# A decoder layer on TensorE: the streamed and the stationary matmul operands are given one address modulo 2048 bytes

## The chip, the core and the metric

The kernel runs on one core of a Trainium2 chip. The metric is the device time of one execution in microseconds (us). Every instruction below is named by its engine (PE is TensorE's matmul, PEld its weight load, DVE VectorE, ACT ScalarE, POOL GpSimd, SP SyncE) and its line in the kernel.

## The reference

One layer on 256 tokens with 2048 channels, all float32. The input is normalised and projected to ten parts; two mixers run side by side, 16-head latent attention with a rotary part, and a short causal convolution; each is widened by a SiLU path, projected back to 2048 channels and weighted by a sigmoid gate computed from the input; the sum goes through one more 2048 x 2048 projection, a norm and the residual.

```python
h = _rmsnorm(x, pre_norm_g)
proj = jnp.einsum('bsd,de->bse', h, w_in)
# split: q_a, c_kv, k_rope, z_mla, c_in, b_gate, c_gate, z_conv, g_mla, g_conv
q  = jnp.einsum('bsr,re->bse', _rmsnorm(q_a, q_a_norm_g), w_q_b)
kv = jnp.einsum('bsr,re->bse', _rmsnorm(c_kv, kv_a_norm_g), w_kv_b)
...
attn = _causal_mla_attention(q_nope, q_rope, k_nope, k_rope, v)
y_mla = jnp.einsum('bse,ed->bsd', attn * silu(z_mla), w_o_mla)
u = c_gate * c_in
conv = sum(conv_w[k] * u_pad[:, k:k + s] for k in range(CONV_K))
y_conv = jnp.einsum('bse,ed->bsd', b_gate * conv * jax.nn.silu(z_conv), w_o_conv)
merged = jax.nn.sigmoid(g_mla) * y_mla + jax.nn.sigmoid(g_conv) * y_conv
out = jnp.einsum('bsd,de->bse', merged, w_out)
return x + _rmsnorm(out, post_norm_g)
```

## The kernel before

**Number format.** A float32 factor is kept as two fp32r parts, a high one (`hi`) and the rest (`lo`), so that one exact product is three matmuls: hi x hi, hi x lo, lo x hi. Activations are stored with both parts side by side: `x_both`, `at_both`, `cv_both` and `m_both` have 16 rows of 512 elements per partition, 256 tokens of the high part and 256 of the low. A row is 2048 bytes. Weights arrive by DMA from SP's queue in units of 128 x 2048 elements (`raw`, three buffers) and are split into `whi` and `wlo`, half a unit (1024 elements, 4096 bytes) at a time, by ACT (line 207) and DVE (line 208), five buffers each.

**Order of the work.** First the input is scaled and split into `x_both` and projected to the latents `qa` and `ckv`. Then comes a loop over 16 heads: five projections of `x_both` per head (`z`, `cg`, `ci`, `b`, `c`), with the attention of the head woven in (`qn`, `kn`, `qr`, `vv`, `sc`, `tp`, `o`). Its results lie in `at_f` and `cv_f`, which are then split into `at_both` and `cv_both`. Then four blocks of 512 output columns (`c` from 0 to 3); in each, four products of 256 tokens by 512 columns are made by `tokens`: two gates from `x_both`, then `at_both` with the attention's output weights, then `cv_both` with the convolution's. Each such product takes 16 rows x 2 halves of the tokens x 3 = 96 matmuls of 512 columns. `features` turns the merged block into `m_both`. Last, four more blocks of 96 matmuls (`out`) multiply `m_both` by the output weights, and each is followed by its part of the norm (`out_block`, `row_norm`, `finish`).

**Which operand streams.** A matmul instruction has a stationary operand, which a weight load brings in before, and a moving one, whose 512 (or 256) columns are then streamed. In `halves`, which makes the heads' projections (lines 202 and 204), the weights are stationary and a whole row of `x_both` streams. In `product` (lines 194 to 196), which makes the `sq` and `out` blocks, it is the other way round: 128 tokens of the activation are stationary (512 bytes per partition) and 512 columns of weights stream (2048 bytes).

```python
def product(ps, a, b, first, last):
    (ah, al), (bh, bl) = a, b
    nc.tensor.matmul(ps, ah, bh, start=first, stop=False)
    nc.tensor.matmul(ps, ah, bl, start=False, stop=False)
    nc.tensor.matmul(ps, al, bh, start=False, stop=last)
```

**Where the tiles lie.** Pools are stacks in each partition's memory: `const` and `wpool` grow from the low end, and `hp`, `cp`, `op` follow on them; `top`, `fp`, `bp`, later `merged_pool` and `dp`, come from the high end down. The size of what is put on first therefore sets the address of all that follows. `LINE` is 32 elements, 128 bytes, and the pads `top_pad` and `const_pad` bring the tiles to multiples of that. The scheduler lays out the order of the instructions on each engine; the weights' buffers come free as the matmuls that read them end.

Of the kernel before, what the change touches and what calls it, by code (L numbers as in the profile page):

```python
# [11 lines left out]
F32 = mybir.dt.float32  # L12
# [6 lines left out]
P = 128  # L19
S = 256  # L20
NT = S // P
# [12 lines left out]
MASKED = -3e38  # L34

UNIT = 2048
LINE = 32
# [41 lines left out]
def tile_layer(ctx: ExitStack, tc: tile.TileContext, xt, x, pos, pvec, post_g, wqa, wi, wkr, wqk, wrv, wsq, out):  # L79
    nc = tc.nc  # L80

    const = ctx.enter_context(tc.tile_pool(name="const", bufs=1))
    top = ctx.enter_context(tc.tile_pool(name="top", bufs=1, side="right"))
    top.tile([P, LINE - 8], F32, name="top_pad")
    wpool = ctx.enter_context(tc.tile_pool(name="wpool", bufs=1))
    psum = ctx.enter_context(tc.tile_pool(name="psum", bufs=1, space=PSUM))

# [131 lines left out]
    make_identity(nc, ident[:, :])  # L219
    ones = const.tile([P, P], F32, name="ones")  # L220
    nc.gpsimd.memset(ones[:, :], 1.0)
    mask = const.tile([P, 3 * P], F32, name="mask")
    nc.gpsimd.memset(mask[:, :], 0.0)
    for o in (0, 2 * P):
        make_causal_mask(nc, mask[:, o : o + P], mask_val=MASKED)
    mhalf = const.tile([P, 1], F32, name="mhalf")
    nc.gpsimd.memset(mhalf[:, :], -0.5)
    hpi = const.tile([P, 1], F32, name="hpi")
# [6 lines left out]
    const.tile([P, LINE - 8], F32, name="const_pad")  # L235
    cos_t = const.tile([P, S], F32, name="cos_t")
    sin_t = const.tile([P, S], F32, name="sin_t")


    main = ctx.enter_context(ExitStack())  # L240
    hp = main.enter_context(tc.tile_pool(name="hp", bufs=1))
    x_both = hp.tile([P, KD, 2 * S], F32R, name="x_both")
    r_x = hp.tile([P, S], F32, name="r_x")
    r_col = hp.tile([P, LINE], F32, name="r_col")[:, :NT]
    fstack = main.enter_context(ExitStack())
    fp = fstack.enter_context(tc.tile_pool(name="fp", bufs=1, side="right"))
    at_f = fp.tile([P, H, S], F32, name="at_f")
# [2 lines left out]
    bp = bstack.enter_context(tc.tile_pool(name="bp", bufs=1, side="right"))  # L250
    qa = bp.tile([P, KR, 2 * S], F32R, name="qa")
    ckv = bp.tile([P, KR, 2 * S], F32R, name="ckv")
    kr = bp.tile([P, 2, S], F32R, name="kr")

    xs = at_f
    angles = [at_f[:, H - 1 - i, :] for i in range(5)]
# [339 lines left out]
    bp = cp  # L596
# [65 lines left out]
    op = ctx.enter_context(tc.tile_pool(name="op", bufs=1))  # L662
# [2 lines left out]
    gb = op.tile([P, D], F32, name="gb")  # L665
    nc.scalar.dma_start(out=gb[:, :], in_=post_g.to_broadcast([P, D]))
    nc.scalar.dma_start(out=xr[:, :, :], in_=x)
    ssq = op.tile([P, NT, LINE // 2], F32, name="ssq")

    def out_products(ps, t, w, kk):  # L670
        ts = slice(t * P, (t + 1) * P)
# [4 lines left out]
    def out_block(c, t, ps):  # L676
        cs = slice(512 * c, 512 * c + 512)
        junk = op.tile([P, 512], F32, name=f"junk{c}_{t}", tag="junk", bufs=2)
        nc.scalar.activation(junk[:, :], ps[:, :], AF.Square, accum_out=ssq[:, t, c : c + 1])
        if c == 3:  # L680
            rr = row_norm(t)
        nc.vector.tensor_tensor(og[:, t, cs], ps[:, :], gb[:, cs], op=ALU.mult)
        return rr if c == 3 else None

    last = []
    part = op.tile([P, LINE], F32, name="part")[:, :NT]

    def row_norm(t):

        ss = op.tile([P, LINE], F32, name=f"fss{t}")[:, :1]  # L690
        nc.vector.scalar_tensor_tensor(
            ss[:, :], ssq[:, t, 3:4], 1.0 / D, part[:, t : t + 1], op0=ALU.mult, op1=ALU.add
        )
        rr = op.tile([P, LINE], F32, name=f"frr{t}")[:, :1]
        nc.gpsimd.tensor_tensor(rr[:, :], ss[:, :], mhalf[:, :], op=ALU.pow)
        return rr

# [111 lines left out]
```

## Time and profile before

| | us |
|---|---|
| median of three runs | 1079.74 |
| the three runs | 1077.57, 1079.74, 1079.75 |
| the profiled execution | 1077.44 |
| its span, first to last instruction | 1075.6 |
| granted TensorE clock over the span | 0.997 |

The span is what the trace shows; 1.8 us of the execution's time lie around it. A row of the profile gives a group of instructions with its count, its busy time and what ended the engine's idle time before it. Ends of matmuls are modelled (a 512-column one is always shown as about 0.39 us long and overlaps the next), so the pace of a stream of matmuls is read from start to start, or from a stretch's length divided by the number of matmuls that start in it.

### The profile page before, as it was taken

To read this page: it belongs to the slowest core of one execution; us is meant where nothing else is said; L and a number is where in the kernel's file an instruction comes from. 1 tells how busy PE (TensorE), PEld (TensorE's weight loads), DVE (VectorE), ACT (ScalarE), POOL (GpSimd) and SP (SyncE) were. 2 spreads that over 40 slices of the span, in tenths; PEclk is the share of its full clock that TensorE was granted. 3 is DMA by queue.
4 is the path that set the end of the run, shared out by engine and by line. 5 is a ranking of instruction groups with operands and counts; after the bars stand their busy time and mean duration, and the time that the engine had idled before them with its cause. 6 is when DMAs were issued, how large, how long until landed. Compare 5 with 4: busy or idle time off the path is not lost.

```text
span 1075.6 us, 14368 instructions
## 1 busy us (share of the span) xinstructions
PE 1056.0 (98%) x5576; PEld 907.3 (84%) x5576; DVE 729.6 (68%) x1132; ACT 586.9 (55%) x849; POOL 47.6 (4%) x70
## 2 busy tenths in 40 slices
PE   9988999999999999999999999999999999999997
PEld 7877798888889889888888878888888888888885
DVE  6999897877877778878787774554455445445562
ACT  7656666666666666666566674334434434434450
POOL 0591000000000000000000000000000000000000
PEclk9999999999999999999999999999999999999998
DMA  8644445454545545545455446555555555557552
GB/s 313 222 146 169 173 161 184 161 195 174 192 169 186 183 160 196 191 152 179 166 194 196 161 161 217 178 190 190 196 195 176 188 187 193 196 194 278 199 189 78
DMA packets 31604, 199.80 MB, mean 186 GB/s; under 512 B 3632, under 2 KB 5296, under 8 KB 9264
## 3 DMA queue, kind: packets, MB, share of 16 engines
q1 hardware_dynamic: 30960, 195.57, 51.4%
q10 hardware_dynamic: 576, 3.31, 0.8%
q8 instruction: 43, 0.70, 0.3%
q14 instruction: 25, 0.20, 0.1%
HBM read 196.78 MB, written 2.10 MB: 185 GB/s over the span
## 4 chain that ended last, share of the span: by engine, by line
PE 86%; DVE 5%; POOL 4%; issue 2%; DMA 2%; ACT 0%; SPq 0%; POOLq 0%; DVEq 0%; ACTq 0%
PE sq L195 11%; PE sq L196 11%; PE sq L194 10%; PE b L202 5%; PE z L202 5%; PE cg L202 5%; PE c L202 5%; PE ci L202 5%; PE c L204 3%; PE b L204 3%; PE ci L204 3%; PE z L204 3%; PE cg L204 3%; PE out L196 2%; PE out L194 2%; PE out L195 2%
## 5 line engine op out<-in xcount | busy, mean ns | idle before, releaser
L208 DVE TENSOR_TENSOR wlo<-raw,whi 128x1024 fp32r<-128x1024 f32 (+1 forms) x372 | 443.0, 1207 | 232.4 <-ACT whi L207 199.0
L207 ACT ACTIVATE whi<-raw 128x1024 fp32r<-128x1024 f32 (+1 forms) x374 | 386.8, 1038 | 338.2 <-PE sq L196 185.5
L195 PE MATMUL sq<-wlo,x_both 128*128 128x512 f32 x256 | 99.7, 390 | 1.6 <-DVE wlo L208 1.6
L196 PE MATMUL sq<-whi,x_both 128*128 128x512 f32 x256 | 99.7, 389 | 0.0
L194 PE MATMUL sq<-whi,x_both 128*128 128x512 f32 x256 | 99.2, 390 | 0.0
L202 PE MATMUL z<-x_both,whi 128*128 128x512 f32 x256 | 61.1, 391 | 2.4 <-DVE f L326 2.4
L202 PE MATMUL b<-x_both,whi 128*128 128x512 f32 x256 | 62.5, 396 | 0.0
L202 PE MATMUL ci<-x_both,whi 128*128 128x512 f32 x256 | 61.5, 392 | 0.0
L202 PE MATMUL cg<-x_both,whi 128*128 128x512 f32 x256 | 61.3, 391 | 0.0
L202 PE MATMUL c<-x_both,whi 128*128 128x512 f32 x256 | 61.1, 391 | 0.0
L195 PEld LDWEIGHTS sq<-wlo,x_both 128*128 128x128 f32 x256 | 48.1, 188 | 11.9 <-DVE wlo L208 2.0
L202 PEld LDWEIGHTS z<-x_both,whi 128*128 128x128 f32 x256 | 47.1, 188 | 11.8 <-issue 2.6
L196 PEld LDWEIGHTS sq<-whi,x_both 128*128 128x128 f32 x256 | 48.1, 188 | 10.0
L194 PEld LDWEIGHTS sq<-whi,x_both 128*128 128x128 f32 x256 | 48.1, 188 | 9.8
L202 PEld LDWEIGHTS b<-x_both,whi 128*128 128x128 f32 x256 | 46.9, 188 | 9.5
L202 PEld LDWEIGHTS c<-x_both,whi 128*128 128x128 f32 x256 | 47.0, 188 | 9.1
L202 PEld LDWEIGHTS cg<-x_both,whi 128*128 128x128 f32 x256 | 46.9, 188 | 9.1
L202 PEld LDWEIGHTS ci<-x_both,whi 128*128 128x128 f32 x256 | 47.0, 188 | 9.1
L196 PE MATMUL sq<-whi,cv_both 128*128 128x512 f32 x128 | 50.5, 395 | 0.0
L194 PE MATMUL sq<-whi,at_both 128*128 128x512 f32 x128 | 50.5, 395 | 0.0
L194 PE MATMUL sq<-whi,cv_both 128*128 128x512 f32 x128 | 50.5, 395 | 0.0
L195 PE MATMUL sq<-wlo,at_both 128*128 128x512 f32 x128 | 50.5, 395 | 0.0
(239 smaller groups left out, 1839.5 us busy)
## 6 DMA issues: line engine op xcount, KB each, us to landing
raw<-wi_dram SPq DMA_DIRECT2D x84, 1024.0 KB, 4.8
raw<-wsq_dram SPq DMA_DIRECT2D x80, 1024.0 KB, 4.8
raw<-wqk_dram SPq DMA_DIRECT2D x8, 1024.0 KB, 4.8
raw<-wrv_dram SPq DMA_DIRECT2D x8, 768.0 KB, 4.1
raw<-wqa_dram SPq DMA_DIRECT2D x8, 256.0 KB, 5.0
raw<-wqa_dram SPq DMA_DIRECT2D x4, 512.0 KB, 7.3
xr<-x_dram ACTq DMA_DIRECT2D x1, 2048.0 KB, 13.3
out_dram<-og SPq DMA_DIRECT2D x6, 256.0 KB, 2.3
```

Source lines behind the costliest of these rows:

```text
L194: nc.tensor.matmul(ps, ah, bh, start=first, stop=False)
L195: nc.tensor.matmul(ps, ah, bl, start=False, stop=False)
L196: nc.tensor.matmul(ps, al, bh, start=False, stop=last)
L202: nc.tensor.matmul(ps[:, :], w[0], both, start=first, stop=False)
L204: nc.tensor.matmul(ps[:, :S], w[1], both[:, :S], start=False, stop=last)
L207: nc.scalar.activation(hi, src, AF.Copy)
L208: nc.vector.tensor_tensor(lo, src, hi.bitcast(F32), op=ALU.subtract)
```

## The change

No instruction is added or removed on any engine but one wait of POOL, and the order on PE, ACT, DVE and SP's queue is the same. What differs is the place of tiles. The mask (1536 bytes) leaves `const` for `bp`, and its memory-set and causal fills on POOL now stand behind the small constants. `r_x` and `r_col` go from `hp` to `const`. The last norm's small tiles (`ssq`, `part`, `fss`, `frr`) go from `op` to `top`, and `top_pad` becomes 480 bytes. With that the addresses within a partition, as the built programs have them, are these:

| tile | before | mod 2048 | mod 512 | after | mod 2048 | mod 512 |
|---|---|---|---|---|---|---|
| `raw`, `whi`, `wlo` (ring) | 21632 on | 1152 | 128 | 21248 on | 768 | 256 |
| `x_both` | 87168 | 1152 | 128 | 86784 | 768 | 256 |
| `at_both` | 121088 | 256 | 256 | 119552 | 768 | 256 |
| `cv_both` | 153856 | 256 | 256 | 152320 | 768 | 256 |
| `m_both` | 196480 | 1920 | 384 | 195328 | 768 | 256 |
| weights of the last `out` block | 132480 on | 1408 | 384 | 131840 on | 768 | 256 |
| `qa`, `ckv`, `kr` | 128256 on | 1280 | 256 | 125568 on | 640 | 128 |
| `qn`, `kn`, `qr`, `vv`, `p` | 161664 on | 1920 | 384 | 160512 on | 768 | 256 |
| `pt` | 193408 | 896 | 384 | 192256 | 1792 | 256 |
| `ident` | 16832 | 448 | 448 | 16832 | 448 | 448 |

```diff
     top = ctx.enter_context(tc.tile_pool(name="top", bufs=1, side="right"))
-    top.tile([P, LINE - 8], F32, name="top_pad")
+    ssq = top.tile([P, NT, LINE // 2], F32, name="ssq")
+    part = top.tile([P, LINE], F32, name="part")[:, :NT]
+    row_s = [top.tile([P, LINE], F32, name=f"fss{t}")[:, :1] for t in range(NT)]
+    row_r = [top.tile([P, LINE], F32, name=f"frr{t}")[:, :1] for t in range(NT)]
+    top.tile([P, 120], F32, name="top_pad")
...
-    mask = const.tile([P, 3 * P], F32, name="mask")
-    nc.gpsimd.memset(mask[:, :], 0.0)
-    for o in (0, 2 * P):
-        make_causal_mask(nc, mask[:, o : o + P], mask_val=MASKED)
     mhalf = const.tile([P, 1], F32, name="mhalf")
...
     sin_t = const.tile([P, S], F32, name="sin_t")
+    r_x = const.tile([P, S], F32, name="r_x")
+    r_col = const.tile([P, LINE], F32, name="r_col")[:, :NT]
...
     x_both = hp.tile([P, KD, 2 * S], F32R, name="x_both")
-    r_x = hp.tile([P, S], F32, name="r_x")
-    r_col = hp.tile([P, LINE], F32, name="r_col")[:, :NT]
...
     kr = bp.tile([P, 2, S], F32R, name="kr")
+    mask = bp.tile([P, 3 * P], F32, name="mask")
+    nc.gpsimd.memset(mask[:, :], 0.0)
+    for o in (0, 2 * P):
+        make_causal_mask(nc, mask[:, o : o + P], mask_val=MASKED)
...
-    ssq = op.tile([P, NT, LINE // 2], F32, name="ssq")
-    part = op.tile([P, LINE], F32, name="part")[:, :NT]
     def row_norm(t):
-        ss = op.tile([P, LINE], F32, name=f"fss{t}")[:, :1]
+        ss, rr = row_s[t], row_r[t]
...
-        rr = op.tile([P, LINE], F32, name=f"frr{t}")[:, :1]
```

## The prediction

> **What bounds the kernel now.** I read the page first: how busy each engine is, the clock, and the chain that ended last.
>
> ```profile
> PE 1056.0 (98%) x5576; PEld 907.3 (84%) x5576; DVE 729.6 (68%) x1132; ACT 586.9 (55%) x849; POOL 47.6 (4%) x70
> PEclk9999999999999999999999999999999999999998
> PE 86%; DVE 5%; POOL 4%; issue 2%; DMA 2%; ACT 0%; SPq 0%; POOLq 0%; DVEq 0%; ACTq 0%
> ```
>
> TensorE is never without work for long, its clock is granted nearly in full throughout, and 86% of the chain is matmuls. So the time is the number of matmuls times their pace, and a change that leaves every engine's instructions and order as they are can only act through the pace of single instructions. The change moves addresses; the question is whether the pace knows of addresses.
>
> Next I cut the second half into its blocks of 96 matmuls, from the first start of one to the first start of the next. The columns are the stretch and its length, PE's busy time (with the rows that touch the stretch, so one or two neighbours are counted too), clock, DMA share and GB/s. First the eight blocks whose stationary operand is `at_both` or `cv_both`:
>
> ```profile
> 667.76:690.07 22.31, 22.31 (x97) 1.00 0.52 188
> 690.07:712.39 22.32, 22.32 (x97) 1.00 0.54 189
> 756.82:779.13 22.31, 22.31 (x97) 1.00 0.53 189
> 779.13:801.45 22.32, 22.32 (x97) 1.00 0.53 188
> 845.88:868.19 22.31, 22.31 (x97) 1.00 0.52 189
> 868.19:890.51 22.32, 22.32 (x97) 1.00 0.54 188
> 934.94:957.25 22.31, 22.31 (x97) 1.00 0.53 189
> 957.25:979.57 22.32, 22.32 (x97) 1.00 0.53 188
> sum 178.52, PE 178.52; mean PE 22.32
> ```
>
> Then blocks of the same shape on `x_both` (the first three) and on `m_both`:
>
> ```profile
> 712.39:734.17 21.78, 21.78 (x98) 1.00 0.56 193
> 801.45:823.23 21.78, 21.78 (x98) 1.00 0.56 194
> 890.51:912.29 21.78, 21.78 (x98) 1.00 0.55 193
> 1002.31:1024.07 21.76, 21.76 (x97) 1.00 0.54 194
> 1024.07:1045.83 21.76, 21.76 (x97) 1.00 0.53 194
> ```
>
> A block on `at_both` or `cv_both` takes 22.31 us, that is 22.31/96 = 232.4 ns a matmul; one on `x_both` 21.78 us (226.9 ns), on `m_both` 21.76 us (226.7 ns). PE is busy without a gap in all of them, at the full clock, on the same instructions with the same shape, and the slow and the fast blocks alternate. The rows of starts show that the difference is in every matmul and not in a wait at some place:
>
> ```profile
> 770.31 0.39 PE L195 MATMUL sq<-wlo,at_both 128*128 128x512 f32 x1
> 770.54 0.39 PE L196 MATMUL sq<-whi,at_both 128*128 128x512 f32 x1
> 770.77 0.39 PE L194 MATMUL sq<-whi,at_both 128*128 128x512 f32 x1
> 770.31 0.19 PEld L196 LDWEIGHTS sq<-whi,at_both 128*128 128x128 f32 x1
> ```
>
> The weight load for the next matmul starts together with the present one (both at 770.31). While one address range streams, another is loaded. So what I look at is their distance: the address of the operand being loaded less that of the one streaming, modulo 512 (successive stationary slices lie 512 bytes apart, so only this remainder is the same for a whole block). From the table of addresses: `x_both` blocks 128 - 128 = 0; `m_both` 384 - 128 = 256; `at_both` and `cv_both` 256 - 128 = 128. Distances 0 and 256 go at 226.7 to 226.9 ns, distance 128 at 232.4.
>
> A third sample comes from the heads, where the weights are the stationary operand. `kn` streams `ckv` while loading `whi`: 128 - 256 = 384 modulo 512. The heads' own projections stream `x_both` at distance 0:
>
> ```profile
> 174.07 1.09 PE L202 MATMUL kn<-ckv,whi 128*128 128x512 f32 x4
> 175.00 0.63 PE L204 MATMUL kn<-ckv,wlo 128*128 128x256 f32 x4
> 175.47 0.28 PE L483 MATMUL sc<-kn,qn_hi 128*128 128x256 f32 x1
> 396.83 3.82 PE L202 MATMUL cg<-x_both,whi 128*128 128x512 f32 x16
> 400.49 2.08 PE L204 MATMUL cg<-x_both,wlo 128*128 128x256 f32 x16
> 402.40 0.86 PE L202 MATMUL ci<-x_both,whi 128*128 128x512 f32 x3
> ```
>
> `kn`: (175.00 - 174.07)/4 = 232.5 ns, as slow as `at_both`. `cg`: (400.49 - 396.83)/16 = 228.8 ns, between the two. The narrow ones (256 columns) go at 0.47/4 = 117.5 ns and 1.91/16 = 119.4 ns: there the distance makes no difference of that kind.
>
> **The change, part by part.**
>
> *`at_both` and `cv_both`* come to distance 256 - 256 = 0 from the weights. Eight blocks of 22.31 become blocks of 21.76 to 21.78: 178.52 - 8 x 21.77 = 4.4 us less, or 178.52 - 8 x 21.78 = 4.3 us; I take 4.3, since `x_both` at distance 0 is the nearest case. The upper bound is 4.4. The lower bound is the pace of `cg`, also at distance 0: 768 x (232.4 - 228.8) = 2.8 us. I take the other end, because the `cg` run follows narrow matmuls and these blocks follow wide ones, as the `x_both` blocks do.
>
> Is the gain passed on to the end? The blocks are PE from end to end, so what is late next would be the weights:
>
> ```profile
> SPq L137 <- DVE wlo L208: 247.6, 48, 5.9
> ACT whi L207 <- PE sq L196: 26.7, 15, 3.1
> raw<-wsq_dram SPq DMA_DIRECT2D x80, 1024.0 KB, 4.8
> ```
>
> SP's queue waits for DVE's split to free a buffer (247.6 us between 712 and 979 us), and ACT waits for PE to free `whi` (26.7 us in two slow blocks). Both are held back by PE, not the reverse, and a unit lands 4.8 us after its issue where a block's quarter lasts 5.4 us. The `x_both` blocks already run at the new pace with the same feed. So all of the 4.3 us reaches the end.
>
> *`x_both`, `m_both`, the last `out` weights.* Distances: `x_both` 0 before and after; `m_both` 256, now 0; the last block 384 - 384 = 0, stays. By the rows of 21.76 and 21.78, 0 to 0.1 us. Taken as 0.
>
> *`qa` and `ckv`* keep a distance: with the weights stationary it goes from 384 to 256 - 128 = 128, and where `ckv` is stationary (`vv`) from 128 to 384. By the rows of 232.4 (128) and 232.5 (384) these are one class: 0. The bounds: `qn`, `kn` and `qr` have 160 wide matmuls; at the fast pace they would save 160 x 5.7 = 0.9 us, and I allow as much the other way, since no row shows this pairing at 128.
>
> ```profile
> L202 PE MATMUL kn<-ckv,whi 128*128 128x512 f32 x64 | 18.3, 399 | 0.6 <-DVE ckv L208 0.5
> L202 PE MATMUL qn<-qa,whi 128*128 128x512 f32 x64 | 17.5, 396 | 0.0
> L202 PE MATMUL qr<-qa,whi 128*128 128x512 f32 x32 | 8.8, 395 | 0.0
> L518 PE MATMUL tp<-ident,p 128*128 128x128 f32 x48 | 8.1, 272 | 0.0
> L629 PE MATMUL mt<-ident,sg 128*128 128x128 f32 x32 | 4.3, 272 | 0.0
> ```
>
> *Transposes* (`tp`, `mt`, 80 of them) go from 384 - 448 = 448 to 256 - 448 = 320, in either role an odd distance before and after: 0, with 80 x 5.7 = 0.5 us either way.
>
> *The mask and the small constants.* POOL's memory-set and two fills of the mask now follow the small constants.
>
> ```profile
> 2.11 0.54 POOL masks.py:30 TENSOR_SCALAR_AFFINE_SELECT mask<-mask 128x128 f32<-128x128 f32 x2
> 2.47 0.20 ACT L231 ACTIVATE warm<-mhalf 128x1 f32<-128x1 f32 x1
> 3.19 0.51 ACT L277 ACTIVATE x_both<-at_f,pv 128x256 fp32r<-128x256 f32 x1 [0.52 <-DMA pv<-pvec_dram]
> ```
>
> ACT's first work waits for the constants' DMA until 3.19 us, after `warm`; the mask is ready at 2.65 us here, and is first read in the heads' loop, behind the whole input stage. 0. *The last norm:* its tiles exist from the start instead of on ground that `cv_both` leaves, so POOL loses a wait for PE that was over long before its wait for DVE. 0.
>
> The sum is -4.3 us, with bounds 4.4 + 0.1 + 0.9 + 0.5 = 5.9 us faster and 2.8 - 0.9 - 0.5 = 1.4 us faster. From the profiled execution's own 1077.44 us that gives 1073.1; from the median of the runs, 1079.74, it gives 1075.4. The four executions lie in two pairs 2.2 us apart; I expect the new median between the two values and write 1074.5.
>
> **The rivals.**
>
> *The address plays no part.* Then the time stays between 1077.4 and 1079.7. [...] The trace does not agree: 22.31 against 21.78 us, eight times over, with nothing else different that I can name. Against that stands that correlation in one execution is all I have; the blocks also differ in their data. 9 in 100.
>
> *A multiple of 256 is what is slow, not the distance.* Before, the slow pairs are those with one operand on a multiple of 256 (`at_both`, `cv_both`, `qa`, `ckv`), and all fast ones are 128 off it. The trace cannot separate this from distance, since no block had both operands on such a multiple. After the change all of them have: the activations, the weights, `m_both`. Then nothing is gained, and every fast wide matmul slows to 232.4 ns: 768 in `sq` on `x_both`, 384 in `out`, 1280 in the heads, 144 in the latents and `kr`, together 2576 x 5.6 = 14.4 us, giving 1091.9 to 1094.1. It decides from 2.2/2576 = 0.9 ns a matmul. For it: the same rows. Against it: `qa` is slow as the streaming operand and `at_both` as the stationary one, which a relation of the two explains with one rule, as it does that distance 256 is fast. 6 in 100.
>
> *Something small that I have not seen eats the gain,* a phase of weight loads as in `cg`, or a later start: about 1077.5. 3 in 100.
>
> **How the numbers follow.** The forecast keeps 82 in 100 and gives 1074.5. Its range goes from the greatest gain below the lower pair, 1077.4 - 5.9 = 1071.5, to 1077.5, the lower pair untouched; that takes in a gain of only 2.8 us from the higher pair, 1079.7 - 2.8 = 1076.9. The measurement can tell about 0.2%, 2.2 us, from no change. Faster by more than that: the forecast, 0.82 with a little of the last rival, 0.83. Same: the first rival and the rest, 0.11. Slower: the second, 0.06.
>
> **What would show it.** Right: the eight blocks last 21.76 to 21.78 us, a sum near 174.2 instead of 178.5; the blocks on `x_both` and `m_both` keep theirs; `kn` keeps 232 ns. Wrong: the eight blocks still last 22.3 us (no part in it), or the `x_both` blocks grow to 22.3 as well (multiples of 256), or they shorten and the span does not follow, with new idle time of PE before them.

## The result and the profile after

| | before | after |
|---|---|---|
| median | 1079.63 us (4 runs, 1077.57 to 1079.75) | 1074.46 us (4 runs, 1073.26 to 1074.65) |
| ratio after to before | | 0.9954, 95% interval 0.9937 to 0.9971 |
| the profiled execution, its span | 1077.44, 1075.6 | 1074.65, 1072.9 |

The kernel became faster by about 0.5%. A later set of five runs of the kernel after, beside nine of before, gave 0.9961 (0.9948 to 0.9975).

The page of after, the same lines as for before (busy time, clock, chain by engine):

```profile
PE 1054.6 (98%) x5576; PEld 909.6 (85%) x5576; DVE 728.8 (68%) x1132; ACT 587.2 (55%) x849; POOL 48.0 (4%) x70
PEclk9999999999999999999999999999999999999999
PE 86%; DVE 5%; POOL 4%; issue 2%; DMA 2%; ACT 0%; SPq 0%; POOLq 0%; DVEq 0%; ACTq 0%
```

Counts and shares are as they were; the bound is the same. The stretches of the eight blocks on `at_both` and `cv_both` in the kernel after (length, PE busy, clock, DMA share, GB/s):

```profile
669.56:691.32 21.76, 21.76 (x97) 1.00 0.55 193
691.32:713.08 21.76, 21.76 (x97) 1.00 0.57 194
757.49:779.25 21.76, 21.76 (x97) 1.00 0.55 194
779.25:801.01 21.76, 21.76 (x97) 1.00 0.56 193
845.43:867.19 21.76, 21.76 (x98) 1.00 0.55 194
867.19:888.95 21.76, 21.76 (x98) 1.00 0.56 193
933.36:955.12 21.76, 21.76 (x98) 1.00 0.54 194
955.12:976.88 21.76, 21.76 (x98) 1.00 0.55 192
sum 174.08, PE 174.08; mean PE 21.76
```

The sum was 178.52 before: 4.44 us less. Blocks on `x_both` (first) and `m_both` (second) of after, and the starts inside a block on `at_both`:

```profile
713.08:734.85 21.77, 21.77 (x98) 1.00 0.55 193
999.59:1021.35 21.76, 21.76 (x97) 1.00 0.56 196
```

```profile
770.64 0.39 PE L199 MATMUL sq<-wlo,at_both 128*128 128x512 f32 x1
770.87 0.39 PE L200 MATMUL sq<-whi,at_both 128*128 128x512 f32 x1
771.09 0.39 PE L198 MATMUL sq<-whi,at_both 128*128 128x512 f32 x1
```

The blocks that hold nothing but their 96 matmuls are now alike, 226.7 ns a matmul, with PE busy from end to end. The gain lies where the prediction put it.

The two profiled spans differ by only 2.8 us although the blocks lost 4.4. The rest lies ahead of them: the execution of after is 1.80 us late at the start of the first of the eight blocks (669.56 us against 667.76). Some 0.5 us of that is lost before `rb_qa` starts (71.61 us against 71.06), and the greater part after it, in the first head, where the clock dips in the execution of after and not in that of before. First before, then after, the same two stretches:

```profile
69.00:92.00 23.00, 18.98 (x111) 1.00 0.37 129
92.00:124.00 32.00, 28.71 (x173) 1.00 0.51 182
```

```profile
69.00:92.00 23.00, 20.01 (x109) 0.93 0.36 126
92.00:124.00 32.00, 28.75 (x157) 0.95 0.52 187
```

A mean clock of 0.93 and 0.95 is two stretches of 3.4 us at half clock, near 72 and 113 us: the granted clock is 0.50 from 71.8 to 75.2 us and from 112.7 to 116.1 us. The first falls on `ci` and is mostly hidden, since `rb_ckv` then waits 0.4 us for DVE instead of 2.0. The second falls on the second head's `z` and costs 1.6 us: its 16 wide matmuls take 117.31 - 111.99 = 5.32 us, in before 115.22 - 111.47 = 3.75. The waits of PE ahead of the two dips are as long as before, to 0.1 us, and the kernel before with a single pad, the first experiment, shows dips in the same two stretches of its profile (mean clock 0.85 and 0.95, over the span 0.993); so I do not put them down to the change. The run named "kept awake" below takes this up.

### The profile page after: what moved, and what is told of

It reads as the page before. It is cut to its first block, busy times and chain, and to the rows that moved or that the text cites. A ratio compares the mean times of both kernels' runs of the same rounds, so it can differ in the third digit from the quotient of the medians.

```text
span 1072.9 us, 14367 instructions
## 1 busy us (share of the span) xinstructions
PE 1054.6 (98%) x5576; PEld 909.6 (85%) x5576; DVE 728.8 (68%) x1132; ACT 587.2 (55%) x849; POOL 48.0 (4%) x70
## 4 chain that ended last, share of the span: by engine, by line
PE 86%; DVE 5%; POOL 4%; issue 2%; DMA 2%; ACT 0%; SPq 0%; POOLq 0%; DVEq 0%; ACTq 0%
PE sq L199 10%; PE sq L200 10%; PE sq L198 10%; PE z L206 5%; PE cg L206 5%; PE ci L206 5%; PE c L206 5%; PE b L206 5%; PE c L208 3%; PE b L208 3%; PE z L208 3%; PE ci L208 3%; PE cg L208 3%; PE out L200 2%; PE out L198 2%
## 5 line engine op out<-in xcount | busy, mean ns | idle before, releaser
L200 PE MATMUL out<-whi,m_both 128*128 128x512 f32 x128 | 49.9, 390 | 0.0
L198 PE MATMUL out<-whi,m_both 128*128 128x512 f32 x128 | 49.9, 390 | 0.0
L199 PE MATMUL out<-wlo,m_both 128*128 128x512 f32 x128 | 49.8, 389 | 0.0
```

## The experiments

**The kernel before, with `at_both` and `cv_both` at distance 256.** One pad of 128 bytes, nothing else of the change.

```diff
+    cp.tile([P, LINE], F32, name="cp_pad")
     at_both = cp.tile([P, H, 2 * S], F32R, name="at_both")
```

Expected: 

> The kernel before with one edit, a pad of 128 bytes ahead of at_both: at_both and cv_both move from 256 to 384 modulo 2048, so their distance from the weights (1152) is 256 modulo 512 and not 0 modulo 2048. Theory A (the pace depends on the distance modulo 256): the eight blocks on at_both and cv_both last 21.76 to 21.78 us instead of 22.31, and the time falls by 4.3 us, the whole gain of the change. Theory B (the same address modulo 2048 is needed): the blocks stay at 22.31 us and the time at 1079.6. Theory C (the blocks are slow for their data, not their place): as B.

Measured: 1074.62 us (5 runs), ratio to before 0.9958 (0.9945 to 0.9970). The first two of the eight blocks and their sum:

```profile
669.45:691.21 21.76, 21.76 (x98) 1.00 0.55 193
691.21:712.97 21.76, 21.76 (x98) 1.00 0.54 194
sum 174.08, PE 174.08; mean PE 21.76
```

The sum is that of the kernel after, to the hundredth. So the whole gain of the change comes from the place of these two tiles, one pad of 128 bytes gives it, and the equal address modulo 2048 isn't needed: a distance of 256 does as well as 0. The moves of the mask, of `r_x` and of the norm's small tiles matter only through the addresses that they set.

**The kernel after, with `x_both` moved off by 128 bytes** and `at_both`, `cv_both` by 256.

```diff
+    hp.tile([P, LINE], F32, name="hp_pad")
     x_both = hp.tile([P, KD, 2 * S], F32R, name="x_both")
...
+    cp.tile([P, LINE], F32, name="cp_pad")
     at_both = cp.tile([P, H, 2 * S], F32R, name="at_both")
```

Expected: 

> The kernel after with x_both moved up by 128 bytes (distance 128 from the weights) and at_both, cv_both moved up by 256 (distance 256); m_both stays at 0. Theory A: the blocks on x_both become slow, 22.31 us instead of 21.78 (eight times 0.53 = 4.3 us more), the heads' 1280 wide matmuls go from 228.8 to about 232.5 ns (4.7 us more), 144 more in the latents add 0.5 us: some 9.5 us more than the kernel after, about 1084; at_both and cv_both stay at 21.76. Theory B: as A, and at_both and cv_both slow as well, about 1088. Theory C: no block changes, about 1074.5.

Measured: 1081.63 us (10 runs), slower than before, ratio 1.0027 (1.0018 to 1.0036). Two blocks on `at_both` and `cv_both`, then one on `x_both`, then a run of a head's matmuls (wide, narrow, and the start of what follows):

```profile
672.32:694.08 21.76, 21.76 (x98) 1.00 0.53 193
694.08:715.84 21.76, 21.76 (x97) 1.00 0.56 194
715.84:738.16 22.32, 22.32 (x98) 1.00 0.52 189
```

```profile
399.01 3.90 PE L206 MATMUL cg<-x_both,whi 128*128 128x512 f32 x16
402.74 2.06 PE L208 MATMUL cg<-x_both,wlo 128*128 128x256 f32 x16
404.64 2.72 PE L206 MATMUL ci<-x_both,whi 128*128 128x512 f32 x11
```

Now it is `x_both` that is slow: 22.32 us a block, and in the head (402.74 - 399.01)/16 = 233.1 ns. The data are those of every other run, so the data are not the cause, and the cost can be moved from one tile to another at will. It holds with the weights in either role, streaming in the blocks, stationary in the heads. The estimate of 1084 was too high. Against the kernel before, with the clock full in both executions, the span is 3.6 us longer; summed from start to start, the blocks on `x_both` give 4.2 us (4.3 were estimated), the heads' wide matmuls 5.2 (4.7), `at_both` and `cv_both` take off 4.3, and the heads' narrow ones, with the waits among them, take off 1.5, which the estimate left out: (404.64 - 402.74)/16 = 118.8 ns against 119.4 before.

**Other distances.** Three at once in the kernel after, by pads ahead of `at_both` and `cv_both` and behind `m_both`; one execution of each (1080.69 and 1080.79 us), read for its blocks alone.

```diff
+    cp.tile([P, 8], F32, name="at_pad")        # second run: 24
     at_both = cp.tile([P, H, 2 * S], F32R, name="at_both")
+    cp.tile([P, 8], F32, name="cv_pad")        # second run: 24
     cv_both = cp.tile([P, KD, 2 * S], F32R, name="cv_both")
...
     m_both = merged_pool.tile([P, KD, 2 * S], F32R, name="m_both")
+    merged_pool.tile([P, 24], F32, name="m_pad")   # second run: 8
```

Expected of the first: 

> The kernel after with three distances modulo 256 at once: at_both 32, cv_both 64, m_both 160 (x_both stays at 0). A look at the block times alone. Theory A, all or nothing: each of the blocks moved off a multiple of 256 lasts about 22.3 us. Theory A, graded: the time grows with the way to the nearest multiple of 256, by the line from 21.77 at 0 to 22.31 at 128: 21.9 for 32, 22.0 for 64, 22.2 for m_both (96 from 256). Theory C: 21.77 everywhere.

Expected of the second: 

> As the run before with at_both at 96, cv_both at 192, m_both at 224 modulo 256. Theory A, all or nothing: about 22.3 us for each. Graded: 22.2 for 96, 22.0 for 192 (64 from 256), 21.9 for 224 (32 from 256). Theory C: 21.77 everywhere.

Measured, a block each on `at_both`, `cv_both` and `m_both`; first at 32, 64 and 160, then at 96, 192 and 224:

```profile
667.87:690.26 22.39, 22.39 (x97) 1.00 0.54 188
690.26:712.66 22.40, 22.40 (x97) 1.00 0.53 188
1003.70:1026.10 22.40, 22.40 (x98) 1.00 0.53 189
```

```profile
669.28:691.77 22.49, 22.49 (x97) 1.00 0.53 187
691.77:713.75 21.98, 21.98 (x97) 1.00 0.55 192
1003.77:1026.17 22.40, 22.40 (x97) 1.00 0.54 189
```

| distance modulo 256 | 0 | 32 | 64 | 96 | 128 | 160 | 192 | 224 |
|---|---|---|---|---|---|---|---|---|
| us for 96 matmuls | 21.76 | 22.39 | 22.40 | 22.49 | 22.31 to 22.32 | 22.40 | 21.98 | 22.40 |
| ns each | 226.7 | 233.2 | 233.3 | 234.3 | 232.4 | 233.3 | 229.0 | 233.3 |

It is not graded: 32 bytes off costs as much as 128. Of these eight only 0 is free, and 192 costs about a third of what 160 and 224 beside it do (0.22 us against 0.64). Neither form of the theory had foreseen 192, and why it is milder stays open. The tiles differ too: 160 and 224 were read on `m_both`, whose distance is 416 and 480 modulo 512 there. That distances 256 apart go alike was seen at 0 and 256, and at 128 and 384 (the `x_both` blocks and the heads of the run above); for the others it was not tried.

**The latents too.** `qa`, `ckv` and `kr` brought to a multiple of 256, with the kernel after run again beside it.

```diff
         make_causal_mask(nc, mask[:, o : o + P], mask_val=MASKED)
+    bp.tile([P, LINE], F32, name="bp_pad")
```

Expected of the kernel after again: 

> The kernel after, unchanged, as the measure for the three runs beside it. 1073.0 to 1074.7, blocks on at_both and cv_both 21.76 us. In its profile the clock tells whether the two stretches at half clock (3.4 us each) near 72 and 113 us are there; with the second the span is about 1072.8, without it about 1071.3.

Expected of the edit: 

> The kernel after with a pad of 128 bytes behind the mask: qa, ckv and kr move from 640 to 512 modulo 2048, so their distance from the weights becomes a multiple of 256. Theory A alone: the 160 wide matmuls of qn, kn and qr go from 232.5 ns to the 228.5 ns of the heads' runs, 0.6 us less in the span. Theory D (the first few wide matmuls after narrow ones are slow at any distance, as the first qa stage shows, which goes at 233 ns at distance 0 in runs of four): qn, kn and qr come in runs of four after narrow ones and stay at 232 to 233 ns, nothing gained. Either is below what the times can tell; the starts in the trace decide.

Measured: 1074.51 us for after (1073.42 to 1075.65), 1074.92 for the edit (1072.80 to 1075.40), no difference that can be told. A run of four wide and four narrow matmuls in the edit:

```profile
175.48 1.09 PE L206 MATMUL qn<-qa,whi 128*128 128x512 f32 x4
176.41 0.64 PE L208 MATMUL qn<-qa,wlo 128*128 128x256 f32 x4
176.88 1.09 PE L206 MATMUL kn<-ckv,whi 128*128 128x512 f32 x4
```

(176.41 - 175.48)/4 = 232.5 ns at a distance of 0 modulo 256: as before. Taken over all such runs of four between 124 and 660 us, start to start, the mean goes from 232.9 ns in the kernel after to 231.4 in the edit: a little is gained, far from 227. So among the distances tried only multiples of 256 reached the pace of 227 ns, and they do not suffice: this run of four behind narrow matmuls goes at 232.5 ns at 0, as `kn` does at 384 in the kernel before. The heads' runs of 16 show where the pace settles. These rows begin with the seventh matmul of the two runs of `cg` shown before, at distance 0 in the kernel before and at 384 with `x_both` moved off:

```profile
398.22 1.98 PE L202 MATMUL cg<-x_both,whi 128*128 128x512 f32 x8
```

```profile
400.41 1.80 PE L206 MATMUL cg<-x_both,whi 128*128 128x512 f32 x7
```

At distance 0 the first six take (398.22 - 396.83)/6 = 231.7 ns each and the last ten (400.49 - 398.22)/10 = 227.0. Off by 128 bytes the last ten stay slow, (402.74 - 400.41)/10 = 233.0 ns. So the slow start and the distance are two effects.

**PE kept awake.** Ten dummy matmuls, whose results are not used, in each of two waits of PE in the first head; then the same with the latents' pad.

```diff
+            with tc.issue_after(latest[0].ins):        # behind the last matmul of kn
+                awake(bank("wake", tag="tp", bufs=1), 10)
             values(h, turn(h, p), sz)
...
         rb = bank(f"rb_{name}", tag="sm", bufs=1)
+        if name == "qa":
+            awake(rb, 10)
```

Expected: 

> The kernel after with ten dummy matmuls of 128x128 put in each of the two waits of PE in the first head (before rb_qa, about 2.7 us, and before the second head's z, about 2.4 us); their results are not used. Theory E (the spread of 2 us between runs comes from the clock, which is halved for 3.4 us when such a wait falls badly): no stretch at half clock between 10 and 1060 us, all runs at the upper clock, the median at about 1072.9 instead of 1074.4, and the spread smaller. Rival (the spread has another source, such as DMA): the same median and spread as the kernel after.

Expected of both: 

> Both edits of the two runs before. Theories A and E: about 1072.3. Theories D and E: about 1072.9, as the dummy matmuls alone. With the rival to E: 1074.4.

Measured: 1074.12 us (1073.81 to 1074.60) and 1074.16 us (1073.48 to 1074.73). The two stretches of the run with the dummies alone, then those of the run with both edits:

```profile
69.00:92.00 23.00, 20.21 (x123) 1.00 0.35 123
92.00:124.00 32.00, 30.37 (x189) 1.00 0.51 187
```

```profile
69.00:92.00 23.00, 20.73 (x116) 0.93 0.35 124
92.00:124.00 32.00, 30.68 (x194) 1.00 0.51 187
```

What PE waits for around them, first with the dummies alone, then in the kernel after:

```profile
PE rb_qa L329 <- DVE dg_qa L320: 2.3, 1, 2.3
PE z L206 <- DVE f L338: 1.2, 1, 1.2
```

```profile
PE rb_qa L321 <- DVE dg_qa L314: 2.8, 1, 2.8
PE z L206 <- DVE f L330: 2.4, 1, 2.4
```

With the dummies alone the clock stays full in the profiled execution; with both edits the first stretch dips to 0.93 all the same. The dummies shorten the first wait only from 2.8 us to 2.3 or 2.4, the second from 2.4 to 1.2, and only the second stretch is without a dip in both. So the expectation of no dip holds in one of two profiles. The five runs with the dummies lie within 0.8 us of each other and the five with both edits within 1.25, where the five of after beside them spread over 2.2 (the first four of after over 1.4). That fits the clock as a source of the spread, but so few runs do not show it. The median did not come down to 1072.9 as expected: the rows put `z` at 112.55 us with the dummies and at 111.99 without, so they cost some of what they save; single runs of after reach 1073.3 without them. None of these versions beats the kernel after beyond what the measurement can tell.

## Why the prediction was right

*The pace knows of the distance between the operand that is loaded and the one that streams.* Shown, in both directions: with one pad the slow blocks become fast (22.31 to 21.76 us), with another the fast ones slow (21.77 to 22.32 us), under the same data and the same order of instructions. The other engines are not what the slow blocks meet: in the trace of before, the 164 matmuls on `at_both` and `cv_both` that ran while ACT, DVE and POOL were all idle last 232 ns on the mean, as do the 465 with one of these at work throughout, and the 289 with the DMA engines under a tenth busy 232.5. What is not separated is whether the streaming operand meets the weights loaded for the next matmul or its own: successive stationary slices lie 512 bytes apart, so both have the same distance here.

*The main term.* 4.3 us was taken, up to 4.4 allowed; the trace has 178.52 - 174.08 = 4.44 us. The lower bound, the heads' 228.8 ns, did not apply: it is the mean of a slow start behind narrow matmuls and a settled pace of 227, as the prediction's reason for passing it over had it, and in these long streams of wide matmuls the pace is 226.7 ns over the whole block. The first rival, no part of the address, is out: the same 96 matmuls take 21.76 or up to 22.49 us by the place of the operand alone. That it is the weight load's read that costs the time was not shown by itself.

*The gain reaches the end.* By the starts of the stretches shown, the kernel after goes from 1.80 us behind at the first of the eight blocks to 2.69 us ahead at the end of the last (976.88 us against 979.57): 0.55 or 0.56 us with each block and at most 0.02 between two pairs of them. The spans end 2.8 us apart, and SP's queue still waits for the buffers:

```profile
SPq L141 <- DVE wlo L212: 244.2, 48, 5.9
```

*The rest at nothing.* `m_both` blocks 21.76 before and after; `qn` and `kn` in the kernel after go as in the run shown above, at 233 ns:

```profile
174.77 1.10 PE L206 MATMUL qn<-qa,whi 128*128 128x512 f32 x4
175.70 0.64 PE L208 MATMUL qn<-qa,wlo 128*128 128x256 f32 x4
```

This came true for another reason than the one given. The prediction read `kn` at 232.5 ns as a third sample for the distance and took 128 and 384 as one class; but the run of four goes at 232.5 ns at distance 0 too, so that sample said nothing about the distance. The main term did not rest on it.

*The second rival,* that a multiple of 256 is slow in itself, fell with the kernel after: there every block has both operands on such a multiple and goes at 226.7 ns.

*The third,* something small that eats the gain, exists: the dip of the clock, 1.6 us where it falls on `z`, in some executions and not in others. The prediction took the pairs of times 2.2 us apart for granted and set its value between them; the cause of the pairs it did not name. Over the 24 runs of the kernel before that stand beside the experiments, the 12 with a mean clock of 0.997 or more have a median of 1078.2 us, the 12 below that 1079.7, which fits the dip.

*The number.* That the median of 1074.46 met the 1074.5 is luck. The four runs of after lie 1.4 us apart, and the two medians differ by 5.17 us where the blocks give 4.44. Why these few runs differ by 0.7 us more stays open; in the later set the medians differ by 4.40 (1078.91 and 1074.51).

## What to carry to other kernels

Where a stream of matmuls runs without gaps, compare the pace of blocks with the same shape: a difference of some per cent at full clock and without waits can be the address (here 22.31 against 21.76 us, 2.5%). Give the streamed and the stationary tiles one address modulo 256 bytes; a pad of 128 bytes did here what the whole rearrangement did (21.76 us a block in both), and a distance of only 32 bytes lost all of it (22.39 us). Here it paid in long runs of wide matmuls (232.4 to 226.7 ns each) and hardly in runs of four between narrow ones (232.9 to 231.4 ns).

## What was not expected of the hardware

- In this kernel a matmul of 128x512 in a long stream takes 226.7 ns when the two operands lie a multiple of 256 bytes apart, and 232 to 234 ns at six of the seven other multiples of 32 that were tried, 229.0 ns at 192.
- After waits of PE of 2.8 and 2.4 us in the first head the granted clock was 0.50 for 3.4 us each time in the profiled execution of after and not in that of before, which has waits of 2.7 and 2.4 us at the same places. What sets the moment of the dip was not shown. Whether filling a wait prevents the dip stays open: with dummies in both waits the clock stayed at 1.00 in one profiled execution and fell to 0.93 over the first stretch in the other.
